# Low halves of weights in pieces of 256 columns, and three small vector instructions made two, in a four-layer transformer kernel

## The chip, the cores and the metric

The kernel runs on one core of a Trainium2 chip. The metric is the device time of one execution in microseconds, the median of three runs. A core has five engines with a queue of instructions each: TensorE (PE; PEld is its weight load), VectorE (DVE), ScalarE (ACT), GpSimd (POOL) and SyncE (SP, which here issues most DMAs). They run side by side and wait for one another through semaphores.

## The reference, cut to what matters

Two layers work on 512 tokens of width 1024 (one with indexed sparse attention and a short convolution, one with latent attention, both with an MLP of width 4096), then two more on 512 tokens and 256 of context: a differential attention with 16 pairs of heads and a neighbourhood attention with 32 heads, whose inner width is 2048. All of it is fp32. Every layer is dominated by products with weights:

```python
x = x + _rms_norm(mix, norm_mix_post[layer])
hn = _rms_norm(x, norm_ffn_pre[layer])
x = x + _rms_norm(_squared_relu_mlp(hn, mlp_w1[layer], mlp_w2[layer]), norm_ffn_post[layer])
```

The differential attention takes the difference of two softmaxes, and norms the result of each head:

```python
p = jax.nn.softmax(s, axis=-1)
p = p.reshape(bsz, n2 // 2, 2, nq, nk)
w = p[:, :, 0] - lam * p[:, :, 1]
o = jnp.einsum('bhqk,bkhe->bqhe', w.astype(v.dtype), v)
...
o = rms_norm(o, subln_g) * (1.0 - lam_init)
return (o.reshape(bsz, n, D_INNER) * jax.nn.silu(z)) @ w_out
```

## The kernel before, in words

Matmuls run on rounded fp32 operands (fp32r). To keep precision, each operand is split into a high half (the value rounded) and a low half (the value minus the high half), and each product is made of three matmuls that add up in PSUM: high by high (L578), low by high (L579 or L580) and high by low.

The weights come as 355 units of up to 1104 columns, in the order in which they are used. `WeightStream` brings them in: SP issues the load of a unit into a ring of three buffers (`w_raw`, L259), ACT rounds it (`w_hi`, L272), and POOL (in five cases DVE) subtracts (`w_lo`, L273), one instruction for the whole unit. The rings of high and low halves hold four units, so the halves may be made up to four units ahead of PE; `tick` makes one more unit at a time, at places that the layers' loops fix. A unit consists of blocks: `n` columns for each of 2 to 8 slices of the contraction, most often four blocks of 256 or eight of 128. PE works through a unit block by block.

The order on every engine is the order in which the code is written. In the two attentions of the second half, loops over steps (`diff_run`, `na_run`) put the attention's stages of neighbouring steps side by side and fill PE between them with pieces of the projections of the next group of heads (`c.fill`).

In the differential attention a step is one tile of 128 queries of one pair of heads. `A` makes the scores of both heads, `B` finds their maxima, `E` takes the exponentials on ACT with their row sums, `Dm` (DVE) forms the difference, `T` transposes it on PE (L2088), `G` multiplies by the values, and after six tiles `Hn` and `H2` norm and gate. `Dm` works without dividing by the first sum: it scales the second exponentials by (first sum × −lam / second sum), and the factor that is left goes into the norm's epsilon, as first sum squared × epsilon (`oe`).

In the neighbourhood attention, `Dm` is a reciprocal of the row sum (L2231) and the product of 512 columns with it (L2232), and PE's transposes (L2239) come next. POOL does other work too: the gates (`SZ`, L1766), the rotation and norms of q and k, low halves of norm outputs (L409 `hl`), and the issue of the DMAs that copy `KH` and `KL` to the other half of the partitions (L1802). L910 and L918 are the index scores of the first layer (matmul, then ACT's relu, then DVE's sum), L730 the normalising step of the first two layers' attentions with L738 its transposes.

Of the kernel before, what the change touches and what calls it, by code (L numbers as in the profile page):

```python
# [12 lines left out]
F32 = mybir.dt.float32  # L13
# [3 lines left out]
OP = mybir.AluOpType  # L17
# [8 lines left out]
EPS = 1e-6  # L26
# [215 lines left out]
class WeightStream:  # L242
# [20 lines left out]
    def split(s, eng=None):  # L263
        nc = s.nc
        u = s.halved
        s.load(u)
        key, nb, n = s.units[u]
        m = nb * n
        raw = s.raw.pop(u)
        hi = s.hi_pool.tile([128, UNIT], F32R, name="w_hi")  # L270
        lo = s.lo_pool.tile([128, UNIT], F32R, name="w_lo")
        nc.scalar.copy(hi[:, :m], raw[:, :m])  # L272
        (eng or nc.gpsimd).tensor_tensor(lo[:, :m], raw[:, :m], hi.bitcast(F32)[:, :m], OP.subtract)  # L273
        s.t[u] = lo, hi
        s.halved += 1
        s.load(u + s.ahead)
# [97 lines left out]
class Net:  # L374
# [1637 lines left out]
    def diff_run(s, c):  # L2012
        nc, X = s.nc, s.X
        QS, KH, KL, SZ, V, yd = c.QS, c.KH, c.KL, c.SZ, c.V, c.yd
        nlam, gs = c.tb["nlam"], c.tb["gs"]
        wt = s.pool("wt", 2)
        ob = s.pool("ob", 2)
        units = [(g, p, t) for g in range(8) for p in range(2) for t in range(6)]
        d, O = {}, {}
# [34 lines left out]
        def E(u):  # L2054
            g, p, t = u
            x = d[u]
            for j in range(2):
                h = 4 * t + 2 * p + j
                S = x["s"][j]
                e = X[ei[0] % 4][:, :S.shape[-1]]  # L2060
                ei[0] += 1
                sm = s.sml.tile([128, 1], F32, name=f"df_s{j}")
                s.act(e, S, AF.Exp, bias=x["nb"][j], scale=-1.0, acc=sm)
                x["e"].append((e, sm))

        def Dm(u):
            g, p, t = u
            x = d[u]
            (ea, sa), (eb, sb) = x["e"]
            rb = s.sml.tile([128, 1], F32, name="df_rb")  # L2070
            nc.vector.reciprocal(rb, sb)
            nc.vector.scalar_tensor_tensor(rb, sa, nlam, rb, OP.mult, OP.mult)
            nc.vector.scalar_tensor_tensor(ea, eb, rb, ea, OP.mult, OP.add)
            if t == 0:
                O[g, p] = ob.tile([128, 6, 128], F32, name="ob"), ob.tile([128, 6], F32, name="oss"), ob.tile([128, 6], F32, name="oe")
            nc.vector.scalar_tensor_tensor(O[g, p][2][:, t:t + 1], sa, EPS, sa, OP.mult, OP.mult)

        def T(u):
            g, p, t = u
# [27 lines left out]
        def Hn(g, p):  # L2107
            o, ss, oe = O[g, p]
            v, y, a = [s.sml.tile([128, 6], F32, name=f"df_{k}") for k in "vya"]
            nc.vector.scalar_tensor_tensor(v, ss, 1.0 / 128, oe, OP.mult, OP.add)  # L2110
            s.act(y, v, AF.Ln)
            s.act(y, y, AF.Exp, scale=-0.5)

            def two():
                nc.vector.tensor_tensor(a, y, y, OP.mult)
                nc.vector.tensor_tensor(a, a, v, OP.mult)
                nc.vector.tensor_scalar(a, a, -0.5, 1.5, OP.mult, OP.add)
                nc.vector.tensor_tensor(y, y, a, OP.mult)
                nc.gpsimd.tensor_tensor(o, o, y.unsqueeze(2).to_broadcast([128, 6, 128]), OP.mult)

            s.defer(two)
# [12 lines left out]
        for i in range(N + HD + 1):  # L2134
# [13 lines left out]
            if u[0]:  # L2148
                E(u[0])
# [6 lines left out]
            if u[0]:  # L2156
                Dm(u[0])
            for _, ev in pcs[1:]:
                ev()
            if u[3] and u[3][2] == 5:  # L2160
                Hn(*u[3][:2])
# [164 lines left out]
```

## Time and profile before

| | before |
|---|---|
| median of three runs | 3223.96 us (3220.66 to 3226.64) |
| profiled execution | 3223.14 us, of which 3221.3 us are the span from the first to the last instruction |
| PE busy | 3067.4 us (95%), 22868 matmuls |
| DVE busy | 2132.6 us (66%) |
| ACT busy | 1605.0 us (50%) |
| POOL busy | 1473.9 us (46%), 1296 instructions; 879.0 us of it the 350 low halves of L273 |
| mean granted clock of PE | 0.989 |

A row of the timeline gives the start and the duration in us, the engine, the line, the instruction, what it writes and reads, its shape, how many were merged, and in brackets how long the engine had been idle and who ended that.

### The profile page before, as it was taken

The numbers are of one execution on the slowest core, as the hardware profiler recorded it, in microseconds if no ns is written. First come the engines' busy times: TensorE is split into PE (matmuls) and PEld (weight loads), VectorE is DVE, ScalarE is ACT, GpSimd is POOL, SyncE is SP. The second block draws the span as 40 slices with busy tenths as digits, with TensorE's granted clock in tenths as the row PEclk, the third lists the DMA queues.
The fourth block names the chain that finished last, engine by engine and source line by source line (L and its number), as shares of the span: only waits on it lengthen the run. The fifth ranks groups of instructions, "written<-read, shape, count | busy, mean of one in ns | idle before, by whom it ended". The sixth has DMA issues, their size and how long they took to land.

```text
span 3221.3 us, 58548 instructions
## 1 busy us (share of the span) xinstructions
PE 3067.4 (95%) x22868; PEld 2882.8 (89%) x22868; DVE 2132.6 (66%) x4241; ACT 1605.0 (50%) x3795; POOL 1473.9 (46%) x1296
## 2 busy tenths in 40 slices
PE   7999999998889999999999999998999999999989
PEld 7888889887788898789999999998999999999988
DVE  4886444556874344656777877788455777777864
ACT  4544533335665333455555555555325555555552
POOL 4432344443333444465544654462355444444444
PEclk9999999999999999999999999999999999999999
DMA  3122333433123344331221222123323322323334
GB/s 122 60 73 73 106 129 126 150 95 99 37 65 107 125 144 136 111 94 52 63 65 60 62 63 65 60 62 95 116 98 97 84 81 75 88 80 89 88 91 138
DMA packets 96128, 291.93 MB, mean 91 GB/s; under 512 B 19166, under 2 KB 28638, under 8 KB 92780
## 3 DMA queue, kind: packets, MB, share of 16 engines
q1 hardware_dynamic: 89148, 259.01, 24.8%
q0 software_dynamic: 5120, 25.17, 3.6%
q10 hardware_dynamic: 1584, 4.00, 0.4%
q8 instruction: 181, 2.97, 0.4%
q14 instruction: 95, 0.78, 0.1%
HBM read 244.05 MB, written 18.92 MB: 82 GB/s over the span
## 4 chain that ended last, share of the span: by engine, by line
PE 49%; DVE 13%; ACT 4%; issue 4%; DMA 3%; POOL 2%; SPq 0%; POOLq 0%; DVEq 0%; ACTq 0%
PE mm L578 13%; PE mm L580 12%; PE mm L579 12%; PE mm L2101 3%; DMA KL<-KL 1%; POOL w_lo L273 1%; PE tp L2239 1%; ACT X L406 1%; PE tp L2088 1%; DVE s L2051 1%; PE mm L2254 1%; PE mm L2249 1%; DVE X L2232 1%; PE s L2040 1%; DVE ge L1765 1%
## 5 line engine op out<-in xcount | busy, mean ns | idle before, releaser
L273 POOL TENSOR_TENSOR w_lo<-w_raw,w_hi 128x1024 fp32r<-128x1024 f32 (+2 forms) x350 | 879.0, 2517 | 1019.7 <-ACT w_hi L272 994.5
L578 PE MATMUL mm<-w_hi,hh 128*128 128x256 f32 (+3 forms) x2880 | 840.0, 292 | 7.9 <-ACT df_sq L406 2.6
L579 PE MATMUL mm<-w_lo,hh 128*128 128x256 f32 (+3 forms) x2880 | 820.3, 285 | 11.3 <-POOL w_lo L273 11.3
L580 PE MATMUL mm<-w_hi,hl 128*128 128x256 f32 (+3 forms) x2880 | 821.3, 285 | 3.3 <-POOL hl L409 3.0
L578 PEld LDWEIGHTS mm<-w_hi,hh 128*128 128x128 f32 x2880 | 550.5, 191 | 19.3 <-ACT df_sq L406 8.5
L579 PEld LDWEIGHTS mm<-w_lo,hh 128*128 128x128 f32 x2880 | 551.2, 191 | 18.4 <-POOL w_lo L273 13.8
L580 PEld LDWEIGHTS mm<-w_hi,hl 128*128 128x128 f32 x2880 | 549.6, 191 | 6.4 <-POOL hl L409 5.5
L272 ACT CAST w_hi<-w_raw 128x1024 fp32r<-128x1024 f32 (+2 forms) x355 | 366.1, 1035 | 206.0 <-PE mm L580 171.3
L578 PE MATMUL mm<-hh,w_hi 128*128 128x256 f32 (+1 forms) x1408 | 455.3, 323 | 3.0 <-DVE M L1083 2.8
L579 PE MATMUL mm<-hl,w_hi 128*128 128x256 f32 (+1 forms) x1408 | 448.3, 318 | 0.6
L580 PE MATMUL mm<-hh,w_lo 128*128 128x256 f32 (+1 forms) x1408 | 446.8, 317 | 1.2 <-DVE w_lo L273 1.2
L578 PEld LDWEIGHTS mm<-hh,w_hi 128*128 128x128 f32 x1408 | 265.9, 189 | 30.9 <-issue 5.2
L579 PE MATMUL mm<-w_lo,gh 128*128 128x256 f32 x1024 | 287.1, 280 | 1.4 <-POOL w_lo L273 1.4
L578 PE MATMUL mm<-w_hi,gh 128*128 128x256 f32 x1024 | 287.6, 281 | 0.0
L580 PE MATMUL mm<-w_hi,gl 128*128 128x256 f32 x1024 | 287.1, 280 | 0.1
L579 PEld LDWEIGHTS mm<-hl,w_hi 128*128 128x128 f32 x1408 | 265.9, 189 | 22.3 <-DVE hl L340 1.7
L580 PEld LDWEIGHTS mm<-hh,w_lo 128*128 128x128 f32 x1408 | 265.6, 189 | 21.9 <-DVE w_lo L273 1.6
L1262 DVE SCALAR_TENSOR_TENSOR macc<-modw,cg,macc 128x1024 f32<-128x1024 f32 x84 | 201.6, 2444 | 29.0 <-DMA modw<-in_mod 29.0
L579 PEld LDWEIGHTS mm<-w_lo,gh 128*128 128x128 f32 x1024 | 193.0, 188 | 1.9 <-POOL w_lo L273 1.6
L578 PEld LDWEIGHTS mm<-w_hi,gh 128*128 128x128 f32 x1024 | 193.3, 189 | 0.4
L580 PEld LDWEIGHTS mm<-w_hi,gl 128*128 128x128 f32 x1024 | 193.0, 189 | 0.5 <-DVE gl L409 0.5
L409 DVE TENSOR_TENSOR gl<-rsq,gh 128x512 fp32r<-128x512 f32 x64 | 45.6, 713 | 220.4 <-ACT gh L406 220.4
(373 smaller groups left out, 6880.4 us busy)
## 6 DMA issues: line engine op xcount, KB each, us to landing
w_raw<-in_w SPq DMA_DIRECT2D x336, 512.0 KB, 3.5
modw<-in_mod SPq DMA_DIRECT2D x24, 1024.0 KB, 5.8
KH<-KH POOLq DMA_DIRECT2D x32, 384.0 KB, 4.0
KL<-KL POOLq DMA_DIRECT2D x32, 384.0 KB, 5.1
xs<-X SPq DMA_DIRECT2D x12, 512.0 KB, 3.1
X<-xs SPq DMA_DIRECT2D x12, 512.0 KB, 6.7
yd<-ob SPq DMA_DIRECT2D x16, 384.0 KB, 2.3
w_raw<-in_w SPq DMA_DIRECT2D x8, 552.0 KB, 4.7
```

Source lines behind the costliest of these rows:

```text
L272: nc.scalar.copy(hi[:, :m], raw[:, :m])
L273: (eng or nc.gpsimd).tensor_tensor(lo[:, :m], raw[:, :m], hi.bitcast(F32)[:, :m], OP.subtract)
L406: return s.nc.scalar.activation(out, in_, func, bias=bias, scale=scale, **kw)
L409: (eng or s.nc.vector).tensor_tensor(lo, x, hi.bitcast(F32), OP.subtract)
L578: mm(ps, ah, bh, start=first, stop=False)
L579: mm(ps, ah, bl, start=False, stop=False)
L580: mm(ps, al, bh, start=False, stop=last)
L1262: nc.vector.scalar_tensor_tensor(acc[:, v], w[:, k2], cv, acc[:, v], OP.mult, OP.add)
L1765: nc.vector.reciprocal(x, x)
L2040: nc.tensor.matmul(o, q, KH[:, h, a:b], start=True, stop=False)
L2051: nc.vector.tensor_tensor_reduce(S, S, s.zero.to_broadcast(list(S.shape)), nrq[:, h:h + 1], 3e38, OP.add, OP.min, nb)
L2101: nc.tensor.matmul(ps, x["w"][:, k], V[g][:, kb, p * 128:(p + 1) * 128], start=k == 0, stop=k == nk - 1)
```

## The change

The subtraction of a unit is no longer one instruction on POOL. It is cut into pieces of a whole number of blocks, `n * max(1, 256 // n)` columns: four of 256 for most units, 276, 288 or 384 where a block is that wide. Where DVE makes the low half it stays one instruction. In `Dm` of the differential attention, the product of the first sum, −lam and 1 / second sum has one tensor operand now, the two other factors are scalars of each partition. The square of the first sum is no longer taken tile by tile: ACT writes the sum straight into its column of `oe`, whose tiles are made in `E`, and `Hn` squares all six columns with one instruction.

```diff
@@ WeightStream.split
-        (eng or nc.gpsimd).tensor_tensor(lo[:, :m], raw[:, :m], hi.bitcast(F32)[:, :m], OP.subtract)
+        w = m if eng else n * max(1, 256 // n)
+        for c in range(0, m, w):
+            c = slice(c, min(m, c + w))
+            (eng or nc.gpsimd).tensor_tensor(lo[:, c], raw[:, c], hi.bitcast(F32)[:, c], OP.subtract)
@@ diff_run, E
-                sm = s.sml.tile([128, 1], F32, name=f"df_s{j}")
+                if j == 0 and t == 0:
+                    O[g, p] = ob.tile([128, 6, 128], F32, name="ob"), ob.tile([128, 6], F32, name="oss"), ob.tile([128, 6], F32, name="oe")
+                sm = s.sml.tile([128, 1], F32, name="df_s") if j else O[g, p][2][:, t:t + 1]
@@ diff_run, Dm
-            nc.vector.scalar_tensor_tensor(rb, sa, nlam, rb, OP.mult, OP.mult)
+            nc.vector.tensor_scalar(rb, sa, rb, nlam, OP.mult, OP.mult)
             nc.vector.scalar_tensor_tensor(ea, eb, rb, ea, OP.mult, OP.add)
-            if t == 0:
-                O[g, p] = ob.tile([128, 6, 128], F32, name="ob"), ob.tile([128, 6], F32, name="oss"), ob.tile([128, 6], F32, name="oe")
-            nc.vector.scalar_tensor_tensor(O[g, p][2][:, t:t + 1], sa, EPS, sa, OP.mult, OP.mult)
@@ diff_run, Hn
+            nc.vector.scalar_tensor_tensor(oe, oe, EPS, oe, OP.mult, OP.mult)
             nc.vector.scalar_tensor_tensor(v, ss, 1.0 / 128, oe, OP.mult, OP.add)
```

On POOL, in the neighbourhood attention where the timeline stands at 2562 us, before: `w_lo` is the low half of a unit, `SZ` a gate, `KH` and `KL` the copies of the keys.

```order
622 L273 TENSOR_TENSOR w_lo<-w_raw,w_hi 128x1024
623 L1766 TENSOR_TENSOR SZ<-SZ,ge 128x128 x2
624 L2194 TENSOR_TENSOR bm_28431<-na,X_66 128x256
625 L273 TENSOR_TENSOR w_lo<-w_raw,w_hi 128x1024
626 L1766 TENSOR_TENSOR SZ<-SZ,ge 128x128
627 L1802 DMA KH<-KH 64x1536
628 L1802 DMA KL<-KL 64x1536
```

And now (lines lie three further down):

```order
620 L276 TENSOR_TENSOR w_lo<-w_raw,w_hi 128x256 x4
621 L1769 TENSOR_TENSOR SZ<-SZ,ge 128x128 x2
622 L2197 TENSOR_TENSOR bm_29071<-na,X_66 128x256
623 L276 TENSOR_TENSOR w_lo<-w_raw,w_hi 128x256 x4
624 L1769 TENSOR_TENSOR SZ<-SZ,ge 128x128
625 L1805 DMA KH<-KH 64x1536
626 L1805 DMA KL<-KL 64x1536
```

Each row of 1024 columns has become four of 256 at the same place; nothing else has moved. Over the whole program POOL's 350 instructions become 1382.

On PE, in the first projection of layer 0 and with the semaphores that each row waits for, before: the matmuls of one unit, three for each of its four blocks.

```order
60 L578 MATMUL mm<-w_hi,hh 128x276 [waits Activation_49]
61 L579 MATMUL mm<-w_lo,hh 128x276 [waits Pool_49]
62 L580 MATMUL mm<-w_hi,hl 128x276
63 L578 MATMUL mm<-w_hi,hh 128x276
64 L579 MATMUL mm<-w_lo,hh 128x276
65 L580 MATMUL mm<-w_hi,hl 128x276
66 L578 MATMUL mm<-w_hi,hh 128x276
67 L579 MATMUL mm<-w_lo,hh 128x276
```

And now:

```order
60 L581 MATMUL mm<-w_hi,hh 128x276 [waits Activation_49]
61 L582 MATMUL mm<-w_lo,hh 128x276 [waits Pool_49]
62 L583 MATMUL mm<-w_hi,hl 128x276
63 L581 MATMUL mm<-w_hi,hh 128x276
64 L582 MATMUL mm<-w_lo,hh 128x276 [waits Pool_49]
65 L583 MATMUL mm<-w_hi,hl 128x276
66 L581 MATMUL mm<-w_hi,hh 128x276
67 L582 MATMUL mm<-w_lo,hh 128x276 [waits Pool_49]
```

The order is the same; the first use of each block waits for POOL, where only the unit's first use did. The matmuls that read a low half and wait for POOL are 1157 now and were 294.

On DVE, at the end of a group of six tiles in the differential attention, before: `df_rb` is the factor, `X` the exponentials, `df_v` the norm's variance.

```order
1380 L2071 RECIPROCAL df_rb<-df_s_16314 128x1
1381 L2072 SCALAR_TENSOR_TENSOR df_rb<-df_s_16312,nlam,df_rb 128x1
1382 L2073 SCALAR_TENSOR_TENSOR X_66<-X_67,df_rb,X_66 128x768
1383 L2076 SCALAR_TENSOR_TENSOR oe<-df_s_16312 128x1
1384 L2110 SCALAR_TENSOR_TENSOR df_v<-oss,oe 128x6
```

And now:

```order
1372 L2076 RECIPROCAL df_rb<-df_s 128x1
1373 L2077 TENSOR_SCALAR df_rb<-oe,df_rb,nlam 128x1
1374 L2078 SCALAR_TENSOR_TENSOR X_66<-X_67,df_rb,X_66 128x768
1375 L2112 SCALAR_TENSOR_TENSOR oe<-oe 128x6
1376 L2113 SCALAR_TENSOR_TENSOR df_v<-oss,oe 128x6
```

The instruction of one column behind `X` has gone from each of the 96 steps, and one of six columns stands in each of the 16 groups. DVE has 3946 rows where it had 4026.

## Rows read from the trace of the kernel before

**Rows 1.** The page: an engine's busy us, share of the span, instructions.

```profile
PE 3067.4 (95%) x22868; PEld 2882.8 (89%) x22868; DVE 2132.6 (66%) x4241; ACT 1605.0 (50%) x3795; POOL 1473.9 (46%) x1296
```

**Rows 2.** Waits of PE by releaser: us in total, times, longest us.

```profile
PE tp L2239 <- DVE X L2232: 27.5, 22, 3.5
PE tp L738 <- DVE X L730: 20.1, 26, 1.5
PE mm L579 <- POOL w_lo L273: 12.7, 11, 2.1
...
PE sp L910 <- ACT relu L406: 8.7, 11, 2.6
PE s L2213 <- DMA KL<-KL: 5.5, 8, 1.4
...
PE mm L580 <- POOL hl L409: 3.0, 6, 0.9
PE tp L2088 <- DVE QS L409: 2.9, 7, 0.4
...
PE tp L1282 <- DVE X L1331: 2.7, 3, 1.6
```

**Rows 3.** Timeline of the neighbourhood attention, 2558 to 2567 us.

```profile
2562.68 2.35 POOL L273 TENSOR_TENSOR w_lo<-w_raw,w_hi 128x1024 fp32r<-128x1024 f32 x1 [0.81 <-ACT w_hi L272]
...
2563.00 2.32 DVE L2232 TENSOR_SCALAR X<-X,na_r 128x512 f32<-128x512 f32 x1
...
2565.46 0.63 PE L2239 MATMUL tp<-ident,X 128*128 128x128 f32 x4 [1.96 <-DVE X L2232]
```

**Rows 4.** Two later waits of L2239; L2232's duration in ns: minimum, median, maximum.

```profile
3054.77 0.63 PE L2239 MATMUL tp<-ident,X 128*128 128x128 f32 x4 [2.98 <-DVE X L2232]
...
3148.63 1.09 PE L2239 MATMUL tp<-ident,X 128*128 128x128 f32 x4 [2.36 <-DVE X L2232]
...
L2232 DVE TENSOR_SCALAR X<-X,na_r x128: 485/489/2621, 2474.6 to 3146.0; 128x512 f32<-128x512 f32 x128
```

**Rows 5.** Timeline, 2582 to 2588 us: four POOL instructions in a row, and DVE.

```profile
2584.30 2.52 POOL L1735 TENSOR_TENSOR st<-st,rq 128x256 f32<-128x256 f32 x4
...
2585.56 0.79 DVE L2232 TENSOR_SCALAR X<-X,na_r 128x512 f32<-128x512 f32 x1
```

**Rows 6.** Timeline, 2417 to 2422 us, POOL.

```profile
2418.42 2.34 POOL L273 TENSOR_TENSOR w_lo<-w_raw,w_hi 128x1024 fp32r<-128x1024 f32 x1
...
2420.72 1.42 POOL L409 TENSOR_TENSOR hl<-nf_f,hh 128x256 fp32r<-128x256 f32 x2
```

**Rows 7.** Span and mean granted clock; then stretches: busy us and instructions.

```profile
core 0: 3221.3 us, clock 0.989
...
core 0: us, PE busy (x) PEld busy (x) DVE busy (x) ACT busy (x) POOL busy (x), PEclk, DMA share, GB/s
515.00:545.00 30.00, 30.00 (x258) 30.00 (x257) 16.45 (x15) 6.30 (x6) 16.35 (x6) 1.00 0.41 137
2824.10:2827.50 3.40, 3.40 (x17) 3.21 (x16) 3.02 (x8) 1.35 (x5) 2.35 (x4) 0.51 1.08 287
3148.40:3151.80 3.40, 3.17 (x15) 3.20 (x16) 0.78 (x2) 1.53 (x2) 2.01 (x3) 0.50 0.68 225
```

**Rows 8.** Timeline of the index scores, 134 to 139 us.

```profile
134.95 2.06 DVE L918 SCALAR_TENSOR_TENSOR am<-relu,wi,am 128x384 f32<-128x384 f32 x1
...
137.76 0.73 PE L910 MATMUL sp<-kih,qi 128*128 128x512 f32 x1 [2.58 <-ACT relu L406]
```

**Rows 9.** Timeline at the end of the differential attention, 2240 to 2256 us.

```profile
2249.68 1.56 DVE L2072 SCALAR_TENSOR_TENSOR df_rb<-df_s,nlam,df_rb 128x1 f32<-128x1 f32 x1
...
2252.45 1.51 PE L2088 MATMUL tp<-ident,X 128*128 128x128 f32 x6 [4.92 <-DVE oe L2076]
```

**Rows 10.** Line 415, a tensor-scalar of 128x2: duration ns minimum, median, maximum.

```profile
L415 DVE TENSOR_SCALAR rs_v<-l1ss x4: 169/170/1680, 756.1 to 783.7; 128x2 f32<-128x2 f32 x4
```

## Prediction

> **What bounds the kernel now.** I read the page's first part, then the waits of PE by releaser, then the timeline at the longest of those waits, and last the granted clock in stretches around them. The page shows PE busy 95% of the span and POOL 46% [rows 1]. PE runs its matmuls in a fixed order, so time can be won only in two places: where PE idles (3221.3 − 3067.4 = 154 us) and where its clock is low. The mean granted clock is 0.989 [rows 7]; as the clock has two levels, that is 0.022 × 3221 = 71 us at half rate.
>
> The waits of PE [rows 2] name the idle time: 27.5 us of it in 22 waits of the neighbourhood attention's transposes (L2239) for the normalised weights that DVE writes at L2232, 20.1 us for the same step of the first two layers (L730), 12.7 us for POOL's low halves of weights (L273), 8.7 us in the index scores of the first layer. The reader is to see in the timeline [rows 3] why L2239 waits: POOL starts a low half of 1024 columns at 2562.68, DVE starts L2232 0.32 us later and takes 2.32 us for it, where the median of that line is 0.489 us [rows 4]. It ends at 2565.32, 0.29 us after POOL's record. PE has idled 1.96 us by then. So a DVE instruction that meets a running POOL instruction sits until that one is through, and the 2.35 us length of the low half is what PE pays.
>
> **The pieces: what a DVE instruction meets.** POOL's price for 256 columns of the same subtraction stands in the trace: two of 128x256 take 1.42 us, 0.71 each, and one of 1024 takes 2.34 [rows 6]. Four pieces take 4 × 0.71 = 2.84 us, 0.5 us more for each of the some 340 weight units. Does DVE get in between two pieces that stand back to back? At 2584.30 POOL runs four instructions of 256 columns in a row, 2.52 us together; DVE's L2232 starts in the midst of them at 2585.56 and takes 0.79 us, 0.30 more than alone, not the rest of the row [rows 5]. It is served at the next end of an instruction, so the wait shrinks from the rest of 2.35 us to the rest of 0.71 us.
>
> (A) Neighbourhood attention. Eight of the 22 waits are like the one shown, 1.9 to 2.4 us long, the first and the last of them at 2565.46 and 3148.63 [rows 3, 4], each with L2232 begun early in a low half. L2232 then ends behind the first piece: each gives back 2.35 − 0.71 = 1.64 us, together 13.1. At 3054.77 (2.98 us [rows 4]) it began late in one; I take 1.4 us for that wait and a short one more. A = −14.5 of 27.5 us. The remaining 13 us are waits that other POOL instructions or the chain itself make.
>
> (B) The same hold in other places. In the index scores L918 takes 2.06 us under a low half, and ACT's next step and PE's matmul behind it wait 2.58 us [rows 8]; four of those eleven waits are of this kind, some 1 us of each goes: −4. Of L730's 20.1 us only a few waits lie under a low half (the longest is 1.5 us [rows 2]): −3. Single ones in the second layer (L1282, 2.7 us) and at the ends of the MLPs: −4. B = −11.
>
> (C) Waits for the low half itself. Before, PE waits for all 1024 columns and then works through four blocks at some 0.38 us; now each block waits for its own 256 columns. The last piece is there 0.5 us later, but only one block is left behind it and not four: 3 × 0.38 − 0.5 = 0.65 us less for each of the 11 waits, and no more than each has: C = −6. The 863 waits that PE gets for it are met long before in most units, and a matmul that carries a met wait is issued like its neighbours: a stretch with waits in it issues 258 matmuls in 30 us [rows 7]. I take nothing for them.
>
> **The vector instructions.** (D) 96 times the last vector step of `Dm` goes, and 16 times one of 128x6 comes. Where `Dm` stands in PE's way it counts: 1.5 us at 2252, where L2072 takes 1.56 us on one element, L2073 follows, and PE's transposes wait 4.92 us for that chain [rows 9]; 0.8 us in the next such row, and most of the 2.9 us in the seven waits for QS [rows 2], where DVE carried L2072 and L2076 just before. D = −5. The new form of L2072 is a tensor-scalar; whether one of 128x1 waits for POOL no row shows. Its bounds are 0.15 us (no wait) and, by the nearest row, a tensor-scalar of 128x2 that took 1.680 us against 0.170 [rows 10], the whole rest of POOL's instruction. I take no wait: the other end costs 1.5 us of D.
>
> The Trainium skill, SBUF — State Buffer, section "Who interferes with whom", speaks against this edit: a tensor-scalar with one SBUF input may run in a two-port mode, and then waits for a POOL instruction as one with two inputs does. The 128x2 row agrees with it. By it D would be −3.5 and the sum 1.5 us higher.
>
> (E) The clock. Behind five of A's eight waits PE has a stretch at the half level: in the first 17 matmuls in 3.40 us at a granted 0.51, in the last 15 at 0.50, against 258 in 30 us (29 in 3.40 us) at 1.00 in a stretch of the MLP where it was never idle [rows 7]. Each such stretch loses some 12 × 0.116 = 1.4 us. The 71 us make about 20 such stretches; the others lie behind other long waits. With the idle time in front cut to 0.3 us I take it that seven go (five of A, two of B and C): E = −10. Bounds: 0 and −20.
>
> (F) What comes later. POOL is 0.5 us later behind each low half and 0.3 us more for each DVE instruction it lets in. Queued behind a low half on POOL are the gates (SZ), the DMAs that copy KH and KL, and the low halves of the norm's output. PE waits eight times for KL (5.5 us) and six times for hl (3.0 us) [rows 2]: 14 × 0.5 = +7. SP's weight loads are issued as much later, three units ahead of use; they are hidden by that lead, and if not they cost 0.5 us a unit.
>
> Sum: −14.5 − 11 − 6 − 5 − 10 + 7 = −39.5. The profiled execution took 3223.14 us, 1.9 over its span and 0.8 below the median of the runs, so 3223.14 − 39.5 = 3183.6, and 3184 beside the median of 3223.96.
>
> **The rivals.** First: the gain is given back at the next wait. PE reaches the following steps earlier, and what does not move with it (KL's copy, ACT's chain of exponentials) ends last there. For it: the waits on KL and hl in [rows 2]; against it: those chains start from PE's own results and move with it. Half of A, B, C and D and all of F are left, E half: −18 − 5 + 7 = −16, 3208 us. Still faster.
>
> Second, slower: POOL becomes what PE waits for. A unit costs POOL 2.84 us and each let-in some 0.3; PE uses up a block in 0.38 us and POOL makes one in 0.71, so wherever the lead of the low halves over PE is used up, each unit costs PE 0.5 us and more. The place is the differential attention, where POOL has the gates and the norms of q and k to do beside the low halves. The price: at 0.5 us for half of the 340 units +85, and with the gain 3269 us. It decides from some 80 units that come too late. Against it: PE waited for a low half 11 times of some 340 [rows 2], and POOL idles for 54% of the span [rows 1].
>
> Third: DVE isn't let in between pieces but waits for all four, so the change doesn't do what it does in A. Each hold grows by 0.5 us, and with 22 + 11 + some 15 waits of PE that is +24: 3247 us. Against it stands the row at 2585.56 [rows 5].
>
> Fourth: nothing is left in sum, as F is twice what I take and E is nothing: within 0.2%.
>
> **How the numbers follow.** Forecast 0.66, with its own range 3166 to 3196 (B, C and E at their ends); given back 0.20; nothing left 0.06; POOL too late 0.05; not let in 0.03. The range that holds 8 in 10 is 3164 to 3211: at the lower end E at −20 and B and C in full (−60), at the upper the first rival with F at +10. A measurement tells 0.2% (6.4 us) from no change. Faster 0.86, same 0.06, slower 0.08.
>
> **What would show it.** Right: pieces of 0.7 us in POOL's record; L2232's longest at 1.2 us and not 2.6; PE's waits for L2232 near 13 us and those for low halves near 7 in more and smaller pieces; the mean granted clock above 0.99; L2076's line gone and the new tensor-scalar near 0.15 us. If it took over 1 us anywhere, the row of 128x2 was the nearer one. Wrong: L2232 still at 2 us and over (third rival), PE's wait for low halves above 12.7 us (second), or a PE that idles as long as before with other names in the list (first).

## The result, and the profile after

The changed kernel takes 3192.07 us (median of four runs, 3190.85 to 3195.2), the kernel before 3224.14 in the same series: a ratio of 0.9903 (95% interval 0.9887 to 0.9919), or 31 us less. The forecast was 3184 (39.5 us less), its range 3164 to 3211.

The page of the changed kernel (columns as in [rows 1]):

```profile
PE 3059.9 (96%) x22868; PEld 2878.8 (90%) x22868; DVE 1909.6 (60%) x4161; ACT 1599.2 (50%) x3795; POOL 1694.0 (53%) x2328
```

The span fell by 30.5 us to 3190.8, the mean granted clock rose from 0.989 to 0.991. PE idles 3190.8 − 3059.9 = 130.9 us of it and not 153.9: 23.0 us were idle time. The other 7.5 are busy time of the same 22868 matmuls. POOL works 220 us more, DVE 223 us less. Most of DVE's busy time that went was waiting inside instructions: the kernel with the pieces alone, the first experiment below, has as many DVE instructions as before (4241) and 195 us less of it.

The place of [rows 3] now, the same weight unit, on POOL, DVE and PE (timeline; columns: start, duration in us, in brackets the idle time before and who ended it):

```profile
2553.76 3.00 POOL L276 TENSOR_TENSOR w_lo<-w_raw,w_hi 128x256 fp32r<-128x256 f32 x4 [0.35 <-ACT w_hi L272]
2553.78 0.99 DVE L2235 TENSOR_SCALAR X<-X,na_r 128x512 f32<-128x512 f32 x1
...
2554.92 0.63 PE L2242 MATMUL tp<-ident,X 128*128 128x128 f32 x4 [0.31 <-DVE X L2235]
```

DVE's product starts 0.02 us behind the first piece, is through after 0.99 us and not 2.32, and PE idles 0.31 us and not 1.96. POOL's four pieces take 3.00 us with it in their midst. Durations over the whole run (ns: minimum, median, maximum):

```profile
L2235 DVE TENSOR_SCALAR X<-X,na_r x128: 485/489/1367, 2465.5 to 3118.4; 128x512 f32<-128x512 f32 x128
...
L2077 DVE TENSOR_SCALAR df_rb<-oe,df_rb,nlam x96: 272/273/277, 1449.9 to 2265.4; 128x1 f32<-128x1 f32 x96
```

The longest product fell from 2.62 us to 1.37. Among the products that begin while a low half is running, the mean fell from 2.06 us (28 of them) to 0.79 (33) and the longest from 2.62 to 1.07; the one of 1.37 began under another instruction of POOL. The new tensor-scalar of one column is never held: 0.272 to 0.277 us, 96 times, 40 of which begin while POOL is running a two-input instruction.

The waits of PE after (releaser: us in total, times, longest), answering to [rows 2]:

```profile
PE tp L741 <- DVE X L733: 17.1, 24, 1.5
...
PE tp L2242 <- DVE X L2235: 12.3, 16, 4.3
PE mm L583 <- POOL hl L412: 6.2, 7, 2.4
PE s L2216 <- DMA KL<-KL: 6.1, 8, 2.5
PE mm L581 <- DVE ot L1956: 5.6, 3, 3.2
...
PE tp L2090 <- DVE X L2078: 5.0, 2, 4.7
...
PE sp L913 <- ACT relu L409: 4.7, 7, 1.3
PE mm L581 <- ACT w_hi L272: 4.4, 3, 2.0
PE mm L582 <- POOL w_lo L276: 4.3, 11, 0.6
...
PE s L2043 <- DMA KH<-KH: 3.2, 1, 3.2
PE tp L1285 <- DVE X L1334: 3.2, 3, 2.3
...
PE mm L581 <- ACT df_sq L409: 2.0, 10, 0.6
...
PE tp L2090 <- DVE KL L412: 1.1, 1, 1.1
...
PE tp L2090 <- DVE oe L2112: 0.5, 1, 0.5
```

And some waits of before that [rows 2] leaves out, since they have changed too:

```profile
PE tp L2088 <- DVE oe L2076: 5.4, 2, 4.9
...
PE tp L2088 <- DVE KL L409: 3.8, 8, 1.9
...
PE mm L578 <- ACT df_sq L406: 2.8, 15, 0.6
...
PE mm L578 <- ACT w_hi L272: 2.6, 2, 1.4
...
PE mm L578 <- DVE ot L1953: 1.3, 2, 0.9
...
PE s L2040 <- DMA KH<-KH: 0.3, 1, 0.3
```

The reader is to see two movements: the waits for vector results and low halves shrank (27.5 to 12.3, 12.7 to 4.3, 8.7 to 4.7, 20.1 to 17.1), and those for what POOL does or lets SP do grew (hl 3.0 to 6.2, KH 0.3 to 3.2, ot 1.3 to 5.6). The second movement is smaller than these pairs say: in a second execution of the kernel before (the last experiment) PE waits 3.6 us for ot and 3.7 for hl, without any piece.

### The profile page after: what moved, and what is told of

The parts are those of the page before. It is cut to its first block, busy times and chain, and to the rows that moved or that the text cites. A ratio compares the mean times of both kernels' runs of the same rounds, so it can differ in the third digit from the quotient of the medians.

```text
span 3190.8 us, 59649 instructions
## 1 busy us (share of the span) xinstructions
PE 3059.9 (96%) x22868; PEld 2878.8 (90%) x22868; DVE 1909.6 (60%) x4161; ACT 1599.2 (50%) x3795; POOL 1694.0 (53%) x2328
## 4 chain that ended last, share of the span: by engine, by line
PE 57%; DVE 6%; POOL 4%; DMA 3%; issue 3%; ACT 3%; SPq 0%; POOLq 0%; DVEq 0%; ACTq 0%
PE mm L581 14%; PE mm L583 14%; PE mm L582 14%; PE mm L2103 3%; POOL w_lo L276 3%; DMA KL<-KL 2%; PE tp L2090 2%; PE tp L2242 2%; PE s L2043 1%; PE s L2044 1%; PE mm L2257 1%; PE mm L2252 1%; PE tp L1781 1%; PE s L2216 1%; DVE X L733 1%
## 5 line engine op out<-in xcount | busy, mean ns | idle before, releaser
L276 POOL TENSOR_TENSOR w_lo<-w_raw,w_hi 128x256 fp32r<-128x256 f32 (+2 forms) x1382 | 1103.4, 831 | 852.1 <-ACT w_hi L272 815.4
L2054 DVE CUSTOM_DVE_ANT_0 s<-s,zero,nrq 128x768 f32<-128x768 f32 (+1 forms) x192 | 158.7, 845 | 18.0 <-PE s L2044 15.3
```

The costliest lines, as they stand in the source:

```text
L276: (eng or nc.gpsimd).tensor_tensor(lo[:, c], raw[:, c], hi.bitcast(F32)[:, c], OP.subtract)
L2054: nc.vector.tensor_tensor_reduce(S, S, s.zero.to_broadcast(list(S.shape)), nrq[:, h:h + 1], 3e38, OP.add, OP.min, nb)
```

## Experiments

Each ratio is to the kernel before, timed in the same series.

**The pieces alone.** The change to `WeightStream.split` without the edits of `diff_run`.

```diff
+        w = m if eng else n * max(1, 256 // n)
+        for c in range(0, m, w): ...
```

> The pieces of 256 columns alone, the vector instructions of the differential attention as in the kernel before. My theory (PE is freed where a vector instruction met a running low half): nearly all of the gain of 31.6 us is here, 28 us, so 3196 us; L2232's longest is 1.4 us and PE's waits for it 12 to 13 us as in the changed kernel; the 1.56 us of L2072 under a low half become some 0.7 us. Rival (the two edits need one another, since a held factor in the differential attention keeps PE late): under 20 us, above 3204 us.

Measured: 3195.93 us against 3224.75, ratio 0.9910 (0.9897 to 0.9924), 29 us less. PE waits 12.0 us for the normalised weights, as expected. The pieces carry nearly all of the gain. One expectation missed: the old factor's longest is still 1.60 us, and PE's wait of 4.9 us behind it stays, for what it meets there is no low half of weights (step D below).

**The vector instructions alone.** The edits of `diff_run`, the low half in one instruction.

```diff
-            nc.vector.scalar_tensor_tensor(rb, sa, nlam, rb, OP.mult, OP.mult)
+            nc.vector.tensor_scalar(rb, sa, rb, nlam, OP.mult, OP.mult)
```

and the edit of the next run.

> The two edits of the differential attention alone, low halves of 1024 columns as before. My theory (step D of the prediction): 5 us less, 3219 us, since L2072 held 1.56 us at 2252 us and the last vector step behind X are off PE's chain. Rival: the next instruction with two SBUF inputs on X takes over the hold, as it waits for the same POOL instruction; then within 1.5 us of before, 3223 us, and X's longest grows by what the factor's loses.

Measured: 3215.80 us, ratio 0.9973 (0.9964 to 0.9981), 9 us less (6 to 12), more than either expectation. With the 29 us of the pieces that makes 38, where both together gave 31: the gains do not add, and between the pieces alone (0.9910) and the changed kernel (0.9903) the intervals show no difference. In DVE's time each of the two expectations has a part. The factor and the product behind it (groups by shape: busy us, mean ns), before and in this kernel:

```profile
L2073 DVE SCALAR_TENSOR_TENSOR X<-X,df_rb,X 128x768 f32<-128x768 f32 x64 | 70.1, 1095 | 2.3
L2072 DVE SCALAR_TENSOR_TENSOR df_rb<-df_s,nlam,df_rb 128x1 f32<-128x1 f32 x96 | 44.1, 459 | 3.5
```

```profile
L2075 DVE SCALAR_TENSOR_TENSOR X<-X,df_rb,X 128x768 f32<-128x768 f32 x64 | 81.6, 1276 | 2.3
L2074 DVE TENSOR_SCALAR df_rb<-oe,df_rb,nlam 128x1 f32<-128x1 f32 x96 | 26.2, 273 | 3.6
```

The factor lost 17.9 us of DVE's time, and the product, which has two SBUF inputs itself, took over 11.5 of it. Where the 9 us come from is asked of the next run.

**Only the square of the sum.** The factor keeps its old form.

```diff
...
+            nc.vector.scalar_tensor_tensor(oe, oe, EPS, oe, OP.mult, OP.mult)   # Hn, once for six tiles
-            nc.vector.scalar_tensor_tensor(O[g, p][2][:, t:t + 1], sa, EPS, sa, OP.mult, OP.mult)   # Dm
```

> The kernel before with one edit of the differential attention: the square of the first sum for six columns at once, once a group, in place of 96 instructions of one column; the factor keeps its form with two SBUF tensor operands, low halves of 1024 columns. Both edits took 9 us off. My theory: this one carries most of it, since what it removes stood behind X on DVE in every step, ahead of the KL, QS and df_sq steps that PE waited for: 7 us, 3217 us. Rival (the factor's hold, which the other edit takes away, carries it): 3 us or less, 3221 us.

Measured: 3218.56 us, ratio 0.9985 (0.9976 to 0.9993), 2 to 8 us less. Between the two expectations, and its interval does not part it from the run with both edits. The waits of PE do tell something. In this kernel:

```profile
PE tp L2087 <- DVE KL L409: 2.1, 1, 2.1
...
PE tp L2087 <- DVE QS L409: 0.3, 1, 0.3
```

Seven of the eight waits for KL and six of the seven for QS went with this edit alone, 1.7 and 2.6 us in all; they are short (0.2 to 0.4 us) and recur about every 107 us as the loop goes from group to group. What of the rest the tensor-scalar carries stays open.

**Pieces only in the neighbourhood attention.**

```diff
-        (eng or nc.gpsimd).tensor_tensor(lo[:, :m], raw[:, :m], hi.bitcast(F32)[:, :m], OP.subtract)
+        w = m if eng or u < 275 else n * max(1, 256 // n)
+        for c in range(0, m, w): ...
```

The vector instructions are those of before.

> Pieces only for the weight units from the neighbourhood attention's first projection on (unit 275 of 355 and later), whole units and the old vector instructions in front of them. My theory (A and the part of E that lies there): the gain of that stretch in the changed kernel stands by itself, 20 us, so 3204 us. Rival (the stretch gains because PE arrives there in another phase after what changed in front): 10 us or less, above 3214 us.

Measured: 3207.68 us, ratio 0.9947 (0.9934 to 0.9959), 17 us less (13 to 21). PE's waits there are 11.6 us in 15. The stretch gains by itself, a little less than I expected; the rival (10 us or less) is out.

**Pieces of 512 and of 128 columns**, in the changed kernel.

```diff
-        w = m if eng else n * max(1, 256 // n)
+        w = m if eng else n * max(1, 512 // n)     # and: m if eng else 128
```

With 512, units whose blocks are 276 or more columns wide keep one block a piece; with 128, a piece need not hold a whole block: a block of 256 columns is made in two.

> The changed kernel with pieces of 512 columns. By 2.34 us for 1024 and 0.71 for 256 a piece of 512 takes 1.25 us, two of them 2.50, 0.34 us less for a unit than four. My theory: a vector instruction that meets a low half waits for the rest of 1.25 us and not of 0.71, so PE's waits for the normalised weights grow from 12.3 to some 16 us, those in the index scores and for low halves by 3 more, and POOL's lateness (hl, KL, KH) falls by 4: 3195 us, L2235's longest 1.9 us. Rival (POOL's lateness is the dearer half, finer pieces cost more than they give): 3187 us or less.

> The changed kernel with pieces of 128 columns, eight for a unit of 1024. From 2.34 us for 1024 and 0.71 for 256 a piece of 128 takes 0.44 us, so a unit 3.5 us, 0.7 more than in four pieces. My theory: the hold shrinks by 0.27 us a piece, 4 us over the waits that are left, and POOL's lateness grows by twice what the pieces of 256 cost, 12 us: 3200 us. Rival (the hold is the dearer half): 3188 us or less.

Measured: with 512 columns 3192.93 us, ratio 0.9905 (0.9891 to 0.9920), the same as with 256. With 128 columns 3222.09, ratio 0.9995 (0.9986 to 1.0004): the whole gain is gone. The product's longest with 512 is 1.53 us and not the 1.9 I expected. The waits of PE with 512, then with 128 columns:

```profile
PE tp L2242 <- DVE X L2235: 18.5, 16, 4.1
```

```profile
PE mm L582 <- POOL w_lo L276: 14.2, 24, 2.4
...
PE tp L2242 <- DVE X L2235: 11.0, 10, 3.9
PE mm L583 <- POOL hl L412: 10.0, 7, 2.6
...
PE s L2043 <- DMA KH<-KH: 4.4, 1, 4.4
```

| columns of a piece | 1024 (before) | 512 | 256 | 128 |
|---|---|---|---|---|
| L2235 begun under a running low half, mean us | 2.06 | 1.09 | 0.79 | 0.56 |
| DVE busy, us | 2132.6 | 1988.2 | 1909.6 | 1870.0 |
| POOL busy, us | 1473.9 | 1576.5 | 1694.0 | 1911.7 |
| PE waits for the normalised weights | 27.5 | 18.5 | 12.3 | 11.0 |
| PE waits for low halves (POOL) | 12.7 | 6.5 | 4.3 | 14.2 |
| median of the runs, us | 3224 | 3192.9 | 3192.1 | 3222.1 |

This is the trade in one row each: PE's wait falls less and less (9.0, 6.2, 1.3 us), POOL's time grows more and more (103, 118, 218 us). I expected 3200 at 128 columns by taking the lateness as twice that of 256; it was far more. Of the 31.6 us that the profiled span is longer than with 256 columns, 17.8 are idle time of PE and 13.8 busy time of the same matmuls; the clock is at its half level for 91.3 us in all, with 256 columns for 61.6. The sign of the prediction's second rival, a wait for low halves above 12.7 us, shows here (14.2) and not at 256; its price does not, since 24 waits of 0.6 us on average are not some 80 late units. Why the lateness grows so fast is not shown.

**Whole units at two places** where the changed kernel lost time.

```diff
+        w = m if eng or 191 <= u < 203 or 265 <= u < 271 else n * max(1, 256 // n)
```

> The changed kernel with whole units at two places where it lost time against the kernel before: the units made from 1335 to 1435 us (end of the second MLP and the first projections of the differential attention, units 191 to 202) and from 2307 to 2352 us (its output projection, 265 to 270). My theory (step F: POOL is late there with hl, the copies of KH and KL and the buffers that SP's loads wait for): PE's waits for hl, KH and ot fall from 6.2, 4.6 and 5.5 us to some 3, 1.4 and 1.4, and with the half-rate stretches behind them 8 to 10 us go: 3183 us. Rival (PE waits there because it arrives earlier, not because POOL is later): the waits stay, 3190 us or more.

Measured: 3184.85 us, ratio 0.9877 (0.9863 to 0.9890). Its waits:

```profile
PE mm L583 <- POOL hl L412: 4.9, 8, 1.3
PE s L2215 <- DMA KH<-KH: 2.7, 1, 2.7
PE mm L581 <- DVE ot L1956: 1.5, 2, 0.9
...
PE s L2043 <- DMA KH<-KH: 0.3, 1, 0.3
```

PE's waits for low halves grew from 4.3 to 6.7. At these places PE had waited because POOL was later, not because PE was earlier: ot went from 5.6 to 1.5, the differential attention's KH from 3.2 to 0.3, hl from 6.2 to 4.9 (less than expected); the neighbourhood attention's KH (L2215) grew from 1.4 to 2.7. For the differential attention's KH the other runs agree: 3.2 to 3.8 us in the four with pieces of 256 there, 0 to 2.5 in the eight with whole units (in one of these, the square of the sum alone, it is 2.5).

**POOL's other long subtraction in pieces**, `hl` of the attentions' inputs.

```diff
-            s.sub_lo(ul[:, b, :qw], y, uh[:, b, :qw], nc.gpsimd if b % 2 else nc.vector)
+            for c in range(0, qw, 256 if b % 2 else qw):
+                c = slice(c, min(qw, c + (256 if b % 2 else qw)))
+                s.sub_lo(ul[:, b, c], y[:, c], uh[:, b, c], nc.gpsimd if b % 2 else nc.vector)
```

> The changed kernel with POOL's other long subtraction in pieces too: the low halves hl of the attentions' inputs (128x768 and 128x512) in pieces of 256 columns. In the changed kernel X of the differential attention at 2235 us is held 2.06 us by one of 128x768 and PE waits 4.67 us for it. My theory: X takes 1.4 us there, PE's wait falls by 0.6 us, and elsewhere POOL's later hl takes back as much: within 2 us of the changed kernel, 3191 us. Rival (the largest holds that are left make the largest waits): 5 us or more below it, 3187 us.

Measured: 3190.53 us, ratio 0.9893 (0.9878 to 0.9908): no more than the changed kernel, as expected, but by another way. The wait for X fell by 2.1 us (5.0 to 2.9), and one of 2.1 us for the norm's variance, which the changed kernel doesn't have, took its place.

**Loads by another queue.**

```diff
-            nc.sync.dma_start(yt[b], yd[8 + b])
+            (nc.scalar if diff and b > 1 else nc.sync).dma_start(yt[b], yd[8 + b])
```

> The changed kernel with six loads of the differential attention's result (yraw, 128x768) issued by ACT instead of SP. In the changed kernel SP issues the load of a weight unit at 2325.02 us, where it waits 4.38 us for a buffer that POOL's pieces free (8 of them in 7.96 us), and the two loads of yraw queued behind it start at 2329.49; PE idles 3.22 us at 2336 behind them and has a stretch at the half level there. My theory (F reaches PE through SP's queue): both go, 4 us less, 3188 us. Rival (the chain over ACT and DVE sets that end): the wait stays, 3192 us.

Measured: 3185.98 us, ratio 0.9881 (0.9868 to 0.9895). The chain that it cuts, in the changed kernel (timeline, 2319 to 2337 us, POOL, SP, ACT and PE):

```profile
2321.08 7.96 POOL L276 TENSOR_TENSOR w_lo<-w_raw,w_hi 128x256 fp32r<-128x256 f32 x8
...
2325.02 4.38 SPq L259 DMA_DIRECT2D w_raw<-in_w  x2
2329.49 0.86 SPq L1941 DMA_DIRECT2D yraw<-yd  x2
...
2333.71 1.78 ACT L409 ACTIVATE yh<-yraw 128x768 fp32r<-128x768 f32 x2 [8.84 <-DMA yraw<-yd]
...
2335.93 0.58 PE L581 MATMUL mm<-w_hi,yh 128*128 128x256 f32 x1 [3.22 <-DVE ot L1956]
```

Eight pieces with DVE's instructions between them take 7.96 us; SP's loads of weights wait for the buffers; the loads of `yraw` stand behind them on SP, then come ACT, DVE and PE. With `yraw` on ACT's queue, PE's waits for ot are:

```profile
PE mm L581 <- DVE ot L1956: 0.3, 1, 0.3
```

But the chain is not new. The same place in the kernel before, and PE's row there in the second execution of that kernel:

```profile
2335.76 5.13 POOL L273 TENSOR_TENSOR w_lo<-w_raw,w_hi 128x1024 fp32r<-128x1024 f32 x2
...
2338.38 2.87 SPq L259 DMA_DIRECT2D w_raw<-in_w  x2
...
2347.94 0.38 PE L578 MATMUL mm<-w_hi,yh 128*128 128x256 f32 x1 [0.47 <-DVE ot L1953]
```

```profile
2354.80 0.39 PE L578 MATMUL mm<-w_hi,yh 128*128 128x256 f32 x1 [2.37 <-DVE ot L1953]
```

Two whole units take 5.13 us, SP is held 2.87 us before the loads of `yraw`, and PE waits 0.47 us in one execution and 2.37 in the other. The pieces add 2.8 us on POOL and 1.5 on SP to a chain that was there; how much of the 6 us this edit would win in the kernel before was not run.

**Both cures together**, and with pieces of 512 columns in front and `hl` in pieces besides.

```diff
+        w = m if eng or 191 <= u < 203 or 265 <= u < 271 else n * max(1, 256 // n)               # both cures
+        w = m if eng or 191 <= u < 203 or 265 <= u < 271 else n * max(1, (512 if u < 275 else 256) // n)   # the second
+            (nc.scalar if diff and b > 1 else nc.sync).dma_start(yt[b], yd[8 + b])               # in each
```

> The changed kernel with both cures of POOL's lateness: whole units at the two places (191 to 202 and 265 to 270) and six loads of yraw issued by ACT. My theory (two separate places, in the traces of the single cures 7 us at 1340 to 1500 and 7 us at 2293 to 2369): they add, 3179 us. Rival (both act on the second place alone): 3185 us, as either of them.

> As the kernel with both cures, and besides pieces of 512 columns in front of the neighbourhood attention (units below 275), 256 in it, and POOL's hl of the attentions' inputs in pieces of 256 columns. My theory: in front of the neighbourhood attention holds are few and POOL's time counts as much as they do, so 512 is worth 0 to 3 us, the pieces of hl 1: 3176 us. Rival (in front the hold counts more): 3182 us or more.

Measured: 3182.34 us, ratio 0.9866 (0.9850 to 0.9882), and 3182.54 us, ratio 0.9872 (0.9858 to 0.9885). The first beats both kernels: its interval lies below that of the changed kernel. It came out between the two expectations and does not decide them: in front of 1339 us, where its instructions are those of the changed kernel, its profile is already 5.9 us later (a matmul that starts at 1339.3 there starts at 1345.2 here), with some 27 us of the clock at its half level against 10. The further edits add nothing that can be measured: 3176 was the theory, and 3182 or more what its rival had named.

**The kernel before once more.**

> The kernel before once more, for one profile. My theory on the clock (step E took each stretch at the half level to belong to the idle time in front of it): the same waits give the same stretches, 18 of them and 71 us within 5. Rival (whether a stretch comes behind a wait differs from one execution to the next): the waits are the same within 1 us in all, but stretches come and go at other places, 5 or more of the 18.

Measured: 3226.49 us in one execution. PE waits 27.7 us for L2232 in 23 waits, and the ten longest are there again (in the first profile from 1.86 to 3.50 us, here from 1.87 to 3.02). Two of these waits with the stretch behind each (columns as in [rows 7]), first in the first profile, where the stretch behind the second is in [rows 7]:

```profile
2651.61 0.63 PE L2239 MATMUL tp<-ident,X 128*128 128x128 f32 x4 [1.95 <-DVE X L2232]
...
2822.80 0.63 PE L2239 MATMUL tp<-ident,X 128*128 128x128 f32 x4 [1.95 <-DVE X L2232]
```

```profile
2651.60:2655.00 3.40, 3.39 (x27) 3.31 (x28) 3.23 (x8) 1.20 (x3) 1.73 (x5) 1.00 0.89 220
```

Then in this one:

```profile
2660.15 0.63 PE L2239 MATMUL tp<-ident,X 128*128 128x128 f32 x4 [1.98 <-DVE X L2232]
...
2831.85 0.63 PE L2239 MATMUL tp<-ident,X 128*128 128x128 f32 x4 [1.93 <-DVE X L2232]
```

```profile
2660.90:2664.30 3.40, 3.40 (x17) 3.21 (x16) 3.02 (x8) 1.91 (x5) 1.79 (x3) 0.50 1.03 253
...
2832.60:2836.00 3.40, 3.19 (x26) 2.89 (x24) 3.02 (x8) 1.90 (x5) 1.79 (x3) 1.00 1.05 273
```

In the first profile the clock stayed at its full level behind the wait at 2651.61 and fell behind the one at 2822.80 ([rows 7]); in this one it is the other way round. Five of the eight waits of step A had such a stretch then, two have one now. The rival is right as to the places: a wait of 1.95 us may or may not be followed by a stretch at the half level. The theory is right as to the sum: over the whole trace the half level takes 71.6 us in 18 stretches in the first profile and 67.5 us in 16 in this one. Not all waits are the same within 1 us: those for ot are 1.3 us in the first and 3.6 here.

## Why the prediction was right, and where it was not

The steps as the prediction named them, and what the traces show (changed kernel minus kernel before, in us; the last column takes the second execution of the kernel before):

| step | forecast | measured | from the repeat |
|---|---|---|---|
| A, normalised weights | −14.5 | −15.2 (27.5 to 12.3) | −15.4 |
| B, other held instructions | −11 | −6.5 (index scores −4.0, L730 −3.0, second layer +0.5) | −6.8 (−5.0, −2.2, +0.4) |
| C, waits for low halves | −6 | −8.4 (12.7 to 4.3, 11 waits as before, the longest 0.6 and not 2.1) | −8.2 |
| D, differential attention | −5 | −6.3 (oe, QS, KL, df_sq and X: 14.9 to 8.6) | −6.4 |
| E, clock | −10 | at most −7.5 (PE's busy time) | at most −9.0 |
| F, POOL later | +7 | +12.8 (hl 3.2, KL 0.6, KH 2.9, ot 4.3, w_hi 1.8) | +10.9 (2.5, 1.3, 3.2, 2.0, 1.9) |
| sum | −39.5 | −31.1 (span −30.5) | −34.9 (span −33.8) |

The forecast's mechanism held and its sum came within 8 us, but in part by luck: the terms miss by 17 us in all, in both directions.

**Right in mechanism and size: A and C.** A vector instruction that meets POOL is served behind the running piece, at the place of [rows 3] and in the sum; the sizes 512 and 128 move the product's time under a low half with the length of a piece (2.06, 1.09, 0.79, 0.56 us). The third rival (not let in) is out. C's sign was as worked out: later last piece, less wait.

**B** was right in kind for the index scores and L730; that both agree to the tenth of a us is chance, as the repeat gives −5.0 and −2.2. The single ones (−4) were not there: the wait for L1331 grew from 2.7 to 3.2.

**D** came out near its forecast by luck, from other terms. The long chain that I priced (4.92 us at 2252) is still 4.7 us. In the changed kernel:

```profile
2231.91 4.33 POOL L412 TENSOR_TENSOR hl<-st,hh 128x768 fp32r<-128x768 f32 x2 [1.87 <-ACT hh L409]
...
2235.00 2.06 DVE L2078 SCALAR_TENSOR_TENSOR X<-X,df_rb,X 128x768 f32<-128x768 f32 x1
```

What held the factor there before is a subtraction of 128x768 (`hl`) that the change leaves whole, not a low half of weights. The new factor is not held, and X inherits the hold: 2.06 us, where it took 1.02 before. What went are the short waits for QS, KL and df_sq in each group, of which I had counted only QS. The upper bound of the tensor-scalar (a hold, by the row of 128x2 in [rows 10]) is out for 128x1. The Trainium skill's rule that spoke against the edit (SBUF — State Buffer, "Who interferes with whom") says that a tensor-scalar can enter a two-port mode, not that each does; these 96 did not wait. No run here shows which of the operands' shapes decides that.

**F failed in size.** I took 0.5 us for each of 14 known waits and wrote that SP's weight loads are "hidden by that lead". The eight waits for KL, priced at 4 us, grew by 0.6 us in all (1.3 from the repeat). The loads were not hidden where another load stands behind them on SP: eight pieces took 7.96 us where two whole units took 5.13, since each let-in vector instruction adds to POOL's 0.5 us a unit, and ot, which was no term of the sum, cost 4.3 us (2.0 from the repeat). KH's copy and hl cost some 3 us each. Whole units at two places took much of this back (hl, KH and ot fell there); their kernel lies 7 us under the changed kernel's median with an interval that just touches its own, and with the loads on ACT's queue besides 10 us under it with an interval clear of it. So part of the loss was the change's own, as far as these waits and intervals go. The loads on ACT's queue alone are no such evidence, since they also cut a wait that the kernel before had.

**E failed in size, and that it is there at all is not shown.** Seven stretches at 1.4 us was read from one profile. The repeat shows that a stretch behind such a wait is a matter of the execution, five of eight once and two of eight another time; and new long waits (KH, ot) had stretches of their own. The half level takes 61.6 us in the changed kernel's profile, 72.7 with the pieces alone and 71.3 with `hl` in pieces too, against 71.6 and 67.5 before: single profiles of kernels with pieces lie on both sides. What part of the 7.5 us is the clock stays open.

**The first rival** (the gain given back, 3208) had its sign from the same waits for hl and KL, but not its reason: with whole units at two places most of them fell again, though PE still comes to both earlier than in the kernel before (the matmuls that stood at 1354.1 and 2309.7 us stand at 1348.7 and 2295.0). Some 4 to 6 us, not half, were given back beyond the 7 forecast. The second (POOL too late) shows its sign, not its price, at 128 columns.

## What to carry to other kernels

Where a vector instruction can be held by another engine's long instruction, the hold is as long as what is left of that instruction; cutting it helps until its fixed cost makes the cutter late, so time two or three sizes and look for the flat part (here 512 and 256 columns). When an engine off the critical path is made slower, follow every queue that waits for its buffers, and what is queued behind the load that waits: price the queue's next entries, not the load itself. Waits that recur in each turn of a loop at 0.3 us can be worth as much as the one long wait that the list of maxima shows. Take a second profile of the kernel before: where a wait differs by 2 us between the two, 2 us of it are not to be put down to the change.

## What the runs showed of the hardware that was not expected

The fall of the clock behind an idle time is not fixed by the program: with the same kernel and waits equal to 0.03 us (1.95 and 1.98, 1.95 and 1.93) the half level came behind the one in one execution and behind the other in another, in a later series; whether both ran on the same chip is not on record. The spans of the two profiles differ by 3.3 us (3221.3 and 3224.6), so a difference of that size between two single profiles need not be the effect of an edit.

A tensor-scalar of 128x1 with two scalars from SBUF took 0.273 us at the median and 0.277 at most in 96 cases, longer than the 0.15 us I took and never held, though 40 of them began under a running instruction of POOL, while the tensor-scalar of 128x2 in [rows 10] took up to 1.680.
